# Two attentions: each pair of heads is divided by its softmax sums and stored in two token halves

## The chip, the core and the metric

The kernel runs on one core of a Trainium2 chip. The metric is the time of one execution in microseconds (us); lower is better. Engines: PE is TensorE, DVE is VectorE, ACT is ScalarE, POOL is GpSimd, SP is SyncE, which here only issues DMA transfers.

## What is computed

The reference is a trunk of two layers over 1024 tokens of width 1024, in float32. Layer 0 mixes tokens by a causal attention with 12 heads of 64 (queries and keys from low-rank projections, with a rotary part of 32); layer 1 by a gated linear recurrence. Both layers also attend with 4 heads of 64 to a bank of 256 memory rows. What matters here:

```python
p = jax.nn.softmax(sc, axis=-1).astype(v.dtype)
return jnp.einsum('bhqk,bkhd->bqhd', p, v)            # causal attention, layer 0
...
mem_out = memory_attention(q_mem, mem_k, mem_v)       # both layers
y = jnp.concatenate([tok, mem_out], axis=-1) * jax.nn.silu(gate)
h = layer_norm(ALPHA * h + y @ w_out[layer], ln_g[layer], ln_b[layer])
```

## The kernel before

Matrices are split into a high and a low part, and a product is three matmuls (high x high, high x low, low x high). Activations lie transposed: 128 features on the partitions, 1024 tokens along the free axis. A pair of heads (2 x 64 features) fills one 128x1024 tile `gt`, which holds SiLU(gate) at first and is multiplied by the attention's output in place.

**Attention units.** `attn_unit` makes one unit: up to 512 queries (one half of the tokens, `c` = 0 or 1) against one block of 128 keys. Its front computes scores on PE (L657, or L765 and L766 for the memory), ACT takes the exponential twice (L561 in full, L562 as the high part `ph`), and L564 subtracts to get the low part `pl`, on POOL, or on DVE for one unit in four and for the last memory head. Its back multiplies by V on PE (L572); a 65th column of ones in V gives the sum of the exponentials. `run_units` lets three units' fronts run ahead of a unit's back, and puts other work between them as fills: the projections of the next pair (L113 to L115, with copies L402 and L403), the pass over the next heads' scores that finds each row's maximum (L454 on PE, L456 and L459 on DVE), and near the end the memory's work (L746, L748). A head of layer 0 has 10 units, 3 of them for the first token half and 7 for the second; a pair of heads has 20. A memory head has 4 units, two for each half.

**Finishing.** After the last unit of a half, `finish_chunk` multiplies the unnormalised output into `gt` (L621, DVE) and copies the row of sums to `den` (L622, ACT). When both halves of both heads of a pair are there, `finish_pair` makes the division: two DMAs spread the sums over 128 partitions (L627), DVE takes reciprocals (L628), two DMAs write them to DRAM (L630), two DMAs read them back, each broadcast over 64 partitions (L633), and POOL multiplies the whole `gt` by them (L634). In layer 0 `gt` is then stored to `y_d` (L665; L773 for the first memory pair) and the next gate is loaded into the tile (L667). There are ten pairs: six of layer 0's attention (0 to 5 below), and two of the memory in each layer.

**Order.** The framework puts the instructions into one queue for each engine, in an order from a planner that simulates the program with estimated costs; an engine works its queue in that order, and an instruction that waits holds up all behind it. SP's queue issues all but a few DMAs. Semaphores follow the data by region.

**Around it.** Layer 0's output projection `out_proj` reads `y_d` back by token blocks of 128 (L835, L947) and takes the last memory pair straight from its tile; layer 1's output projection reads the tiles in SBUF.

Of the kernel before, what the change touches and what calls it, by code (L numbers as in the profile page):

```python
# [10 lines left out]
F32 = mybir.dt.float32  # L11
# [4 lines left out]
ALU = mybir.AluOpType  # L16
# [4 lines left out]
S = 1024  # L21
# [23 lines left out]
def hybrid_kernel(ctx: ExitStack, tc: tile.TileContext, io):  # L45
    nc = tc.nc
    PE, ACT, DVE, POOL, SP = nc.tensor, nc.scalar, nc.vector, nc.gpsimd, nc.sync

    main = ctx.enter_context(tc.tile_pool(name="main", bufs=1))
    small = ctx.enter_context(tc.tile_pool(name="small", bufs=2))  # L50
# [192 lines left out]
    y_d = dram.tile([8, 128, S], F32, name="y_d")  # L243
# [9 lines left out]
    HALF = [slice(0, 512), slice(512, 1024)]  # L253
# [243 lines left out]
    den = pb[1].tile([128, S], F32, name="den")  # L497
    den_d = dram.tile([16, 2, S], F32, name="den_d")
# [4 lines left out]
    def vview(t):  # L503
        return t.rearrange("p (s e d) -> p s e d", s=8, e=2)
# [113 lines left out]
    def finish_chunk(gt, e, c, ops):  # L618
        cs = slice(c * 512, (c + 1) * 512)
        y = gt[e * 64:(e + 1) * 64, cs]  # L620
        DVE.tensor_tensor(out=y, in0=ops[0:64, :], in1=y, op=ALU.mult)  # L621
        ACT.copy(den[32 * e:32 * e + 1, cs], ops[64:65, :])  # L622

    def finish_pair(gt, slot):
        rn = small.tile([128, 16], F32, tag="rn", name="rn")
        for e in range(2):
            SP.dma_start(rn[:, e * 8:(e + 1) * 8], den[32 * e:32 * e + 1, :].rearrange("o (a b) -> o a b", a=128))  # L627
        DVE.reciprocal(rn, rn)  # L628
        for e in range(2):
            SP.dma_start(den_d[slot, e].rearrange("(a b) -> a b", a=128), rn[:, e * 8:(e + 1) * 8])  # L630
        rec = Of[slot % 2]
        for e in range(2):
            SP.dma_start(rec[e * 64:(e + 1) * 64, :], den_d[slot, e:e + 1, :].broadcast_to([64, S]))  # L633
        POOL.tensor_tensor(out=gt, in0=gt, in1=rec, op=ALU.mult)  # L634

    SC = 1.0 / math.sqrt(96.0)

    def main_head(h):
        kh_, kl_, qh_, ql_ = sets[h % 4]
        p, e = h // 2, h % 2  # L640
        vh, vl = vview(VH[p % 3]), vview(VL[p % 3])
        gt = GA[p % 4]
        out_units = []
        for c in range(2):
            ops = bank[3 + c]
            units = [([(j, 0, 512, 0)], 512, []) for j in range(4 * c)]
            j = 4 * c
            units.append(([(j, 0, 512, 0)], 512, [0]))
            units.append(([(j + 1, 0, 384, 128), (j + 3, 384, 128, 384)], 512, [0, 384]))
            units.append(([(j + 2, 0, 256, 256)], 256, [0]))  # L650
            for ui, (tl, n, blocks) in enumerate(units):
                def scores(ps, tl=tl, c=c):
                    for (j, c0, w, q0) in tl:
                        ks = slice(j * 128, (j + 1) * 128)
                        qs = slice(c * 512 + q0, c * 512 + q0 + w)
                        for i, (k, q, r) in enumerate(((kh_, ql_, 96), (kl_, qh_, 96), (kh_, qh_, 97))):
                            yield lambda: PE.matmul(ps[:, c0:c0 + w], k[0:r, ks], q[0:r, qs],  # L657
                                                    start=(i == 0), stop=(i == 2))
                last = ui == len(units) - 1

                def post(c=c, ops=ops):
                    finish_chunk(gt, e, c, ops)
                    if c == 1 and e == 1:
                        finish_pair(gt, p)
                        SP.dma_start(y_d[p], gt)  # L665
                        if p < 4:
                            SP.dma_start(gt, gate_d[p])  # L667
                out_units.append(attn_unit(scores, n, SC, blocks,
                                           [(vh[:, j, e, :], vl[:, j, e, :], c0, w, q0) for (j, c0, w, q0) in tl],
                                           ui == 0, last, ops, post if last else None))  # L670
        return out_units
# [82 lines left out]
    def mem_main(m, q1, q2, KH, KL, VmH, VmL, slot, gts, opsb):  # L754
        vh = VmH[:, 0:520].rearrange("p (t h d) -> p t h d", t=2, h=4)
        vl = VmL[:, 0:520].rearrange("p (t h d) -> p t h d", t=2, h=4)
        gt = gts[m // 2]
        out_units = []
        for c in range(2):
            ops = opsb[(2 * m + c) % len(opsb)]  # L760
            qs = slice(c * 512, (c + 1) * 512)
            for kt in range(2):
                def scores(ps, kt=kt, qs=qs):
                    ks = slice(m * 256 + kt * 128, m * 256 + (kt + 1) * 128)
                    yield lambda: PE.matmul(ps, KH[:, ks], q1[:, qs], start=True, stop=False)  # L765
                    yield lambda: PE.matmul(ps, KL[0:65, ks], q2[0:65, qs], start=False, stop=True)  # L766

                def post(c=c, ops=ops):
                    finish_chunk(gt, m % 2, c, ops)
                    if m % 2 == 1 and c == 1:  # L770
                        finish_pair(gt, slot + m // 2)
                        if slot == 6 and m == 1:
                            SP.dma_start(y_d[6], gt)  # L773
                out_units.append(attn_unit(scores, 512, 0.125, [], [(vh[:, kt, m, :], vl[:, kt, m, :], 0, 512, 0)],
                                           kt == 0, kt == 1, ops, post if kt == 1 else None, m == 3))
        return out_units
# [329 lines left out]
    den = pd[1].tile([128, S], F32, name="den1")  # L1106
# [112 lines left out]
```

## Time and profile before

| | us |
|---|---|
| median of 3 runs | 925.75 (925.34 to 928.98) |
| the profiled execution, whole | 924.84 |
| its span, first to last instruction | 923.0 |
| PE busy in the span | 896.5 |
| DVE, ACT, POOL busy | 592.2, 443.1, 222.9 |

Layer 0's attention with the memory lies at 220 to 514 us of the span, layer 1's memory attention at about 745 to 816 us. A line of a timeline has start, duration, engine, line, operation, tile written<-tiles read, shapes, a count xN of merged instructions, and in brackets the idle time before it and what ended it. A busy PE is a modelled figure: consecutive matmuls overlap, so the distance between starts says more than the durations.

### The profile page before, as it was taken

How to read it: one execution, taken by the hardware profiler on the slowest of the kernel's cores; microseconds unless marked ns; L12 is line 12 of the kernel's file. 1: busy time of each engine (PE TensorE's matmuls, PEld its weight loads, DVE VectorE, ACT ScalarE, POOL GpSimd, SP SyncE). 2: the span in 40 equal slices, each digit the busy share in tenths (PEclk: the TensorE clock that was granted, in tenths of full speed). 3: DMA queues.
4: the chain of work that ended last, by engine and by line, in shares of the span. 5: the costliest groups of instructions: out<-in, count | busy, mean ns of one | idle time of the engine just before them, and what ended most of it. 6: DMA issues, size and time to landing. Idle time of an engine off the chain costs nothing.

```text
span 923.0 us, 12452 instructions
## 1 busy us (share of the span) xinstructions
PE 896.5 (97%) x4477; PEld 735.2 (80%) x4477; DVE 592.2 (64%) x1207; ACT 443.1 (48%) x764; POOL 222.9 (24%) x219
## 2 busy tenths in 40 slices
PE   9999999999999999999999999988999999999996
PEld 8998888877787788778777888867888877678886
DVE  7953346258867767796775497646997154457655
ACT  4422311217676667777795122107997156753000
POOL 5100023101526364563672200000000032210000
PEclk9999999999999999999999999998999999999998
DMA  9103133314022213056657653111113921252411
GB/s 328 45 15 109 55 100 127 128 63 111 23 61 70 59 58 104 13 144 178 194 150 207 197 194 125 50 51 47 45 46 113 220 69 47 69 184 91 155 73 46
DMA packets 45945, 96.08 MB, mean 104 GB/s; under 512 B 10906, under 2 KB 20282, under 8 KB 45884
## 3 DMA queue, kind: packets, MB, share of 16 engines
q1 hardware_dynamic: 45308, 94.47, 32.7%
q8 instruction: 35, 0.57, 0.3%
q10 hardware_dynamic: 576, 0.82, 0.3%
q14 instruction: 26, 0.21, 0.1%
HBM read 71.94 MB, written 23.16 MB: 103 GB/s over the span
## 4 chain that ended last, share of the span: by engine, by line
PE 82%; DVE 7%; ACT 3%; issue 3%; DMA 2%; POOL 2%; SPq 0%; DVEq 0%; ACTq 0%; POOLq 0%
PE bank L113 10%; PE bank L115 10%; PE bank L114 10%; PE bank L858 6%; PE bank L860 6%; PE bank L859 6%; PE bank L572 6%; PE bank L657 5%; PE bank L367 3%; PE bank L369 3%; PE bank L368 3%; PE bank L154 2%; PE bank L155 2%; PE bank L153 2%; PE bank L454 2%
## 5 line engine op out<-in xcount | busy, mean ns | idle before, releaser
L564 POOL TENSOR_TENSOR pl<-Pf,ph 128x512 fp32r<-128x512 f32 (+1 forms) x99 | 124.6, 1268 | 116.4 <-ACT ph L562 93.6
L561 ACT ACTIVATE Pf<-bank 128x512 f32<-128x512 f32 (+1 forms) x152 | 86.3, 568 | 50.3 <-DVE bank L558 20.8
L657 PE MATMUL bank<-st,st 96*128 96x512 f32 (+7 forms) x432 | 105.5, 342 | 0.1
L90 DVE TENSOR_TENSOR R<-wf,R 128x1024 fp32r<-128x1024 f32 (+4 forms) x43 | 48.8, 1138 | 65.6 <-POOL R L82 59.8
L657 PEld LDWEIGHTS bank<-st,st 96*128 96x128 f32 (+1 forms) x432 | 75.7, 189 | 13.0 <-DVE st L403 0.5
L562 ACT ACTIVATE ph<-bank 128x512 fp32r<-128x512 f32 (+1 forms) x136 | 76.2, 561 | 0.2
L82 POOL TENSOR_SCALAR R<-wf 128x1024 fp32r<-128x1024 f32 (+3 forms) x25 | 24.4, 979 | 200.1 <-PE bank L114 97.3
L113 PE MATMUL bank<-R,R 128*128 128x256 f32 (+1 forms) x190 | 63.2, 333 | 0.7 <-ACT Pf L375 0.4
L114 PE MATMUL bank<-R,R 128*128 128x256 f32 (+1 forms) x190 | 62.3, 328 | 0.1
L115 PE MATMUL bank<-R,R 128*128 128x256 f32 (+1 forms) x190 | 62.2, 327 | 0.0
L456 DVE CUSTOM_DVE_ANT_0 bank<-bank,cmask 128x384 f32<-128x384 f32 (+3 forms) x96 | 48.8, 517 | 9.8 <-PE bank L454 9.0
L123 ACT ACTIVATE rq_t<-lnv 128x1 f32<-128x1 f32 x16 | 3.3, 203 | 101.7 <-DVE lnv L909 101.7
L367 PE MATMUL bank<-xh,R 128*128 128x512 f32 x128 | 50.8, 397 | 0.1
L369 PE MATMUL bank<-xh,R 128*128 128x512 f32 x128 | 50.7, 396 | 0.0
L368 PE MATMUL bank<-xl,R 128*128 128x512 f32 x128 | 50.5, 395 | 0.0
L572 PE MATMUL bank<-ph,VH 128*65 128x512 f32 (+2 forms) x144 | 49.2, 342 | 0.0
L572 PE MATMUL bank<-pl,VH 128*65 128x512 f32 (+2 forms) x144 | 44.8, 338 | 2.2 <-POOL pl L564 1.2
L572 PE MATMUL bank<-ph,VL 128*65 128x512 f32 (+2 forms) x144 | 47.0, 337 | 0.0
L859 PE MATMUL bank<-wo,yh 128*128 128x512 f32 (+1 forms) x126 | 46.8, 371 | 0.0
L858 PE MATMUL bank<-wo,yh 128*128 128x512 f32 (+1 forms) x126 | 46.6, 369 | 0.0
L860 PE MATMUL bank<-wo,yl 128*128 128x512 f32 (+1 forms) x126 | 46.0, 369 | 0.0
L904 DVE SCALAR_TENSOR_TENSOR GA<-GA,bank 128x512 f32<-128x512 f32 (+1 forms) x34 | 22.0, 647 | 37.1 <-PE bank L860 37.1
(315 smaller groups left out, 2447.1 us busy)
## 6 DMA issues: line engine op xcount, KB each, us to landing
wf<-w SPq DMA_DIRECT2D x26, 512.0 KB
wf<-wout SPq DMA_DIRECT2D x16, 512.0 KB
Of<-den_d SPq DMA_DIRECT2D x20, 256.0 KB
GA<-x SPq DMA_DIRECT2D x8, 512.0 KB
h_d<-GA SPq DMA_DIRECT2D x8, 512.0 KB
GA<-h_d SPq DMA_DIRECT2D x8, 512.0 KB
y_d<-GA SPq DMA_DIRECT2D x7, 512.0 KB
out<-GA SPq DMA_DIRECT2D x7, 512.0 KB
```

The costliest lines, as they stand in the source:

```text
L113: PE.matmul(out, lh, rh, start=(i == 0), stop=False)
L114: PE.matmul(out, lh, rl, start=False, stop=False)
L115: PE.matmul(out, ll, rh, start=False, stop=(i == n - 1))
L367: PE.matmul(ps[n], hi[:, ks], xh[k][:, cs], start=(k == 0), stop=False)
L369: PE.matmul(ps[n], lo[:, ks], xh[k][:, cs], start=False, stop=(k == 7))
L561: ACT.activation(pf[:, :n], ps[:, :n], AF.Exp, scale=scale)
L564: lo_eng.tensor_tensor(out=lo[:, :n], in0=pf[:, :n], in1=f32(hi)[:, :n], op=ALU.subtract)
L572: mm.append(lambda: PE.matmul(ops[0:65, q0:q0 + w], st, mv[:, c0:c0 + w], start=start, stop=stop))
L657: yield lambda: PE.matmul(ps[:, c0:c0 + w], k[0:r, ks], q[0:r, qs], start=(i == 0), stop=(i == 2))
L858: PE.matmul(out, hi, woh[k][:, ns], start=(k == ko[0]), stop=False)
L859: PE.matmul(out, hi, wol[k][:, ns], start=False, stop=False)
L860: PE.matmul(out, lo, woh[k][:, ns], start=False, stop=(k == ko[7]))
```

## The change

`finish_pair` becomes `finish_half`, called after each half of the pair's second head, for that half alone. All six DMAs, the reciprocal and the multiply act on half the tokens, and the store to `y_d` too; the gate load after it stays whole and comes after the second half.

```diff
-    def finish_pair(gt, slot):
-        rn = small.tile([128, 16], F32, tag="rn", name="rn")
+    def finish_half(gt, slot, c):
+        cs = HALF[c]
+        rn = small.tile([128, 8], F32, tag="rn", name="rn")
         for e in range(2):
-            SP.dma_start(rn[:, e * 8:(e + 1) * 8], den[32 * e:32 * e + 1, :].rearrange("o (a b) -> o a b", a=128))
+            SP.dma_start(rn[:, e * 4:(e + 1) * 4], den[32 * e:32 * e + 1, cs].rearrange("o (a b) -> o a b", a=128))
         DVE.reciprocal(rn, rn)
         for e in range(2):
-            SP.dma_start(den_d[slot, e].rearrange("(a b) -> a b", a=128), rn[:, e * 8:(e + 1) * 8])
+            SP.dma_start(den_d[slot, e, cs].rearrange("(a b) -> a b", a=128), rn[:, e * 4:(e + 1) * 4])
         rec = Of[slot % 2]
         for e in range(2):
-            SP.dma_start(rec[e * 64:(e + 1) * 64, :], den_d[slot, e:e + 1, :].broadcast_to([64, S]))
-        POOL.tensor_tensor(out=gt, in0=gt, in1=rec, op=ALU.mult)
+            SP.dma_start(rec[e * 64:(e + 1) * 64, cs], den_d[slot, e:e + 1, cs].broadcast_to([64, 512]))
+        eng = POOL
+        eng.tensor_tensor(out=gt[:, cs], in0=gt[:, cs], in1=rec[:, cs], op=ALU.mult)
...
                     finish_chunk(gt, e, c, ops)
-                    if c == 1 and e == 1:
-                        finish_pair(gt, p)
-                        SP.dma_start(y_d[p], gt)
-                        if p < 4:
+                    if e == 1:
+                        finish_half(gt, p, c)
+                        SP.dma_start(y_d[p][:, HALF[c]], gt[:, HALF[c]])
+                        if c == 1 and p < 4:
                             SP.dma_start(gt, gate_d[p])
...
                     finish_chunk(gt, m % 2, c, ops)
-                    if m % 2 == 1 and c == 1:
-                        finish_pair(gt, slot + m // 2)
+                    if m % 2 == 1:
+                        finish_half(gt, slot + m // 2, c)
                         if slot == 6 and m == 1:
-                            SP.dma_start(y_d[6], gt)
+                            SP.dma_start(y_d[6][:, HALF[c]], gt[:, HALF[c]])
```

## Rows read from the trace of the kernel before

**Rows 1.** The page's part 1: each engine's busy us, share, instructions.

```profile
PE 896.5 (97%) x4477; PEld 735.2 (80%) x4477; DVE 592.2 (64%) x1207; ACT 443.1 (48%) x764; POOL 222.9 (24%) x219
```

**Rows 2.** Windows: bounds, length, busy time by engine, granted clock, DMA share, GB/s.

```profile
238.00:514.00 276.00, 269.73 (x1526) 219.04 (x1525) 199.58 (x452) 196.84 (x372) 138.98 (x122) 1.00 0.38 111
...
800.00:840.00 40.00, 38.75 (x166) 30.09 (x165) 26.12 (x26) 24.74 (x30) 4.61 (x2) 1.00 0.52 174
```

**Rows 3.** Timeline of PE: matmuls that PE stood idle before, and some neighbours.

```profile
315.93 0.39 PE L454 MATMUL bank<-st,st 96*128 96x256 f32 x1 [0.96 <-DVE mx L459]
...
409.78 0.39 PE L572 MATMUL bank<-ph,VL 128*65 128x512 f32 x1
411.16 0.44 PE L572 MATMUL bank<-pl,VH 128*65 128x512 f32 x1 [1.00 <-POOL pl L564]
...
448.39 0.44 PE L572 MATMUL bank<-pl,VH 128*65 128x512 f32 x1 [1.04 <-POOL mx L741]
...
462.42 0.39 PE L572 MATMUL bank<-ph,VL 128*65 128x512 f32 x1
462.65 0.39 PE L572 MATMUL bank<-pl,VH 128*65 128x512 f32 x1
...
485.76 0.44 PE L572 MATMUL bank<-pl,R 128*65 128x512 f32 x1 [1.07 <-POOL pl L564]
...
802.65 0.45 PE L572 MATMUL bank<-mpl,VH 128*65 128x512 f32 x1 [1.25 <-DVE mpl L564]
```

**Rows 4.** The division's multiply, L634, by source line: min/median/max ns.

```profile
L634 POOL TENSOR_TENSOR GA<-GA,Of x8: 2389/2404/2416, 277.2 to 512.8; 128x1024 f32<-128x1024 f32 x8
```

**Rows 5.** Timeline of POOL in layer 0's attention, and at 800 us.

```profile
262.20 1.30 POOL L564 TENSOR_TENSOR pl<-Pf,ph 128x512 fp32r<-128x512 f32 x1 [5.41 <-ACT ph L562]
...
407.49 2.39 POOL L634 TENSOR_TENSOR GA<-GA,Of 128x1024 f32<-128x1024 f32 x1
409.84 3.94 POOL L564 TENSOR_TENSOR pl<-Pf,ph 128x512 fp32r<-128x512 f32 x3
...
428.15 1.30 POOL L564 TENSOR_TENSOR pl<-Pf,ph 128x512 fp32r<-128x512 f32 x1 [3.47 <-ACT ph L562]
...
461.17 3.76 POOL L564 TENSOR_TENSOR pl<-Pf,ph 128x512 fp32r<-128x512 f32 x3 [2.02 <-PE bank L572]
...
479.83 2.41 POOL L634 TENSOR_TENSOR GA<-GA,Of 128x1024 f32<-128x1024 f32 x1 [3.25 <-issue]
...
799.67 2.39 POOL L634 TENSOR_TENSOR GB<-GB,Of 128x1024 f32<-128x1024 f32 x1 [6.86 <-DMA Of<-den_d]
```

**Rows 6.** Timeline of ACT: sums copied after a second head's first half; end of layer 0.

```profile
250.31 0.58 ACT L622 COPY den<-bank 1x512 f32<-1x512 f32 x1
...
458.75 0.58 ACT L622 COPY den<-bank 1x512 f32<-1x512 f32 x1
...
515.26 0.50 ACT L84 CAST R<-GA 128x128 fp32r<-128x128 f32 x2 [1.33 <-POOL GA L634]
```

**Rows 7.** Timeline of SP's queue over pair 3's division.

```profile
396.54 0.55 SPq L627 DMA_DIRECT2D rn<-den  x1
399.26 0.81 SPq L630 DMA_DIRECT2D den_d<-rn  x2
400.72 1.13 SPq L633 DMA_DIRECT2D Of<-den_d  x2
...
409.91 0.33 SPq L665 DMA_DIRECT2D y_d<-GA  x1
```

**Rows 8.** The reciprocal, L628, by source line: durations, then DVE's idle time before.

```profile
L628 DVE RECIPROCAL rn<-rn x10: 235/252/253, 269.7 to 809.1; 128x16 f32<-128x16 f32 x10
...
  DMA rn<-den: 6.3, 5
```

**Rows 9.** Timeline of DVE: a reciprocal of pair 1, and layer 1's memory.

```profile
315.28 0.25 DVE L628 RECIPROCAL rn<-rn 128x16 f32<-128x16 f32 x1 [0.81 <-DMA rn<-den]
...
800.55 2.65 DVE L564 TENSOR_TENSOR mpl<-Pf,mph 128x512 fp32r<-128x512 f32 x2 [1.79 <-ACT mph L562]
```

## The prediction

> **What bounds the kernel now.** I read the page first, then windows over the two stages that the diff touches, then PE's timeline in them for the places where PE stands idle, and at each of these the timelines of POOL, DVE, ACT and SP for the instruction that was late.
>
> The page shows one engine at its limit: PE is busy 897 of 923 us, and no other above 64% [rows 1]. In the stage from 238 to 514 us PE is idle 276.00 - 269.73 = 6.3 us, and in the 40 us around the end of layer 1's memory attention 1.25 us, at a granted clock of 1.00 in both, the level of 2.4 GHz [rows 2]. So whatever the change does to POOL, DVE or SP, it gains at most these 7.5 us (0.8%), and it costs only where it makes PE wait anew. The question is which of these idle stretches hang on the division of a pair.
>
> Matmuls of 512 columns follow each other at 0.23 us (462.42 and 462.65), though each is drawn 0.39 long [rows 3]. So a stall costs the distance of starts less 0.23: at 411.16 it is 411.16 - 409.78 - 0.23 = 1.15 us, 0.15 more than the idle time in brackets. Read in the same way, the stalls that stand next to a division are 1.15 (pair 3), 1.19 (pair 4, 448.39), 1.22 (pair 5, 485.76), 1.40 (layer 1, 802.65) and 1.11 (pair 1, 315.93) [rows 3]. Together 6.1 us.
>
> They have three causes. In pairs 3, 4 and 5 the matmul waits for a low part that POOL made late, and before it in POOL's queue stands the multiply L634: 407.49 for 2.39 us, then three low parts without a break; 479.83 for 2.41 us [rows 5]. In layer 1 the low part is DVE's: the first of two takes 2.65 - 0.69 = 1.96 us, while POOL's multiply runs from 799.67 to 802.06 [rows 5, 9]. In pair 1 it is DVE's reciprocal, which waits 0.81 us for its sums to land, with the maximum pass behind it on DVE [rows 9].
>
> **The change, part by part.**
>
> *The second half's multiply is half as long.* It stays where the whole one was, and lasts about 1.3 us in place of 2.40 [rows 4]; the nearest row is a POOL tensor_tensor of 128x512, 1.30 us [rows 5]. A low part queued behind it comes 1.1 us earlier. That takes 1.1 us from each of the stalls of pairs 3, 4 and 5, which leaves 0.05 to 0.12 of each: -3.3 us. The bounds are -3.6 (the stalls go whole, because the broadcasts land earlier too) and 0 (the planner puts the multiply elsewhere, and other low parts wait behind it).
>
> *Layer 1.* The multiply splits into two of 1.3 us. The first half's sums are there some 4 us earlier, so its multiply falls before the busy stretch; the second would run from about 799 to 800.3 and be over before DVE's low part at 800.55. The bounds are -1.4 and 0; I take -1.0, since a low part may still meet the end of a POOL instruction. The Trainium skill, page "SBUF — State Buffer", section "Who interferes with whom", says that a DVE instruction with two SBUF inputs and a GpSimd instruction that reads SBUF exclude each other for a whole instruction. By that rule DVE's low part would be held until 802.06 and end at 802.75, which the trace supports roughly (it ended near 802.5); halves would shorten one such hold but offer twice as many, and by it alone this term would lie anywhere between its bounds.
>
> *The first half's multiply, new, ten times.* Where does it fall? The chain from the last DMA of the sums to the multiply took 407.49 - 396.54 = 10.9 us in pair 3 [rows 5, 7]; with halves I reckon some 10. The second head's first half is complete at unit 15 of 20: its sums are copied by 250.9 in pair 0 [rows 6], so the multiply is due near 261, and there POOL has nothing to do for 5.41 us, as PE is busy with the next pair's projections and no exponentials come [rows 5]. Pairs 1 to 4 have the same hole, the last and shortest one 3.47 us before 428.15 [rows 5]. The multiply costs nothing there: the cover is the hole, and without it it would cost its own 1.3 us each. Pair 5 has no such hole: its sums are copied by 459.3 [rows 6], and after 461.17 POOL makes three low parts in one go, the first of them done at about 462.5, 0.2 us before the matmul that wants it at 462.65 [rows 3, 5]. The multiply comes near 470, where the margins are still thin. I take +0.8 us, between 0 (it slips behind the next fill) and 2.4 (it costs its length and waits another 1.1 us on a late broadcast). In the memory pairs of layer 0 POOL is idle around the divisions, so 0.
>
> *The reciprocal, ten more on DVE.* Each lasts 0.25 us and may wait for its sums at the head of DVE's queue; behind it stand the maximum pass and the low parts. Of ten so far five waited, 6.3 us in all [rows 8], and one cost PE anything, 1.11 us. Ten more would cost +1.0 on the same rate. The bounds are 0 and 10 x 1.1 = +11.
>
> *Issues on SP, 60 more and 7 more stores.* About 0.5 us each; the six of a division occupy SP for 0.55 x 2 + 0.81 + 1.13 = 3.0 us of some 13 [rows 7]. SP also stands still between them until each step has landed. What is queued behind are weights and rotary rows for the next pair, which it wants several us later. PE has no stall of note that ends on such a load now. I take 0, up to +2.
>
> *End of layer 0.* The last pair's multiply ends at 515.2, and ACT waited 1.33 us for it [rows 6]. PE did not stop there, because three token blocks were prepared ahead. An earlier first half only adds margin: 0.
>
> The sum is -3.3 - 1.0 + 0.8 + 1.0 = -2.5 us, from the profiled 924.84 to 922.3. The median of the runs lies 0.9 us above that execution, so 923.2.
>
> **The rivals.**
>
> *Every stall goes and nothing new comes.* Then -3.6 - 1.4 - 1.1 (pair 1's reciprocal no longer meets the maximum pass) = -6.1, which gives 919.6. For it: POOL's holes lie just where the first halves fall. Against it: it needs luck on DVE in ten new places.
>
> *The waits only move.* The second half's chain still has all its legs, so POOL still stands at the multiply until the broadcast lands (3.25 us idle before 479.83 [rows 5]), and the planner, which does not know the real landing times, puts a low part behind each of the two. If half of the gain goes that way (-2.1) and pair 5 and DVE cost 2.4 and 1.5, the time is 924.84 + 0.9 + 1.8 = 927.5.
>
> *Slower: the reciprocals block DVE.* The new ones come at units 15 to 19 of a pair, where the maximum pass uses DVE most, and each stands at the head of the queue until a DMA has landed, as at 315.28 [rows 9]. At 1.1 us each, ten cost 11 us against gains of 4.3, and the time is 932.4. It decides from about 0.9 us each. Against it: nine of ten cost PE nothing so far. The Trainium skill, page "DMA: Bandwidth & Descriptors", section "Rules for kernel authors", says that many small transfers should be joined into a large one, since below 64 KB one pays mostly overhead. Here the sums' transfers of 4 KB become 2 KB, so by that rule each half would wait about as long as the whole did, and there would be twice as many waits; no run so far shows the half.
>
> **How the numbers follow.** Chances: the forecast 0.50, every stall gone 0.20, the waits move 0.18, the reciprocals 0.12. A measurement of this kernel tells about 0.5% (4.6 us) from no change. The forecast's own range, 921.1 to 926, and the moved waits lie within it; only the first rival is below 921.1, only the last above 930.4: faster 0.20, same 0.68, slower 0.12. The range runs from the first rival's 919.6 to 929, the moved waits' time with SP's share added to it, and leaves the last rival out.
>
> **What would show it.** Twenty multiplies at about 1.3 us; the first halves' multiplies of pairs 0 to 4 in the holes after the pair's last low part; PE's stalls near 411, 448 and 486 gone or below 0.2, and the one near 802 smaller; one new stall near 465 to 472. The prediction is wrong if stalls stay as long with a multiply half as long (then the landing, not POOL's work, set them), if PE stalls before L454 behind reciprocals in more than two or three pairs, or if SP's queue delays weights so that L113 waits.

## The result

The changed kernel is slower: a median of 940.71 us (938.63 to 942.90, 4 runs) against 927.17 for the kernel before on the same chip (4 runs), a ratio of 1.0146, 95% interval 1.011 to 1.0183. The prediction was 923.2, range 919.6 to 929.0: wrong in sign, and outside its range. The profiled execution took 938.63 us, span 936.8, 13.8 more than before.

The page of the changed kernel, part 1 and the count of DMA packets (45945 before):

```profile
PE 902.3 (96%) x4477; PEld 737.2 (79%) x4477; DVE 592.3 (63%) x1217; ACT 442.5 (47%) x764; POOL 221.8 (24%) x229
...
DMA packets 54314, 96.09 MB, mean 103 GB/s; under 512 B 17098, under 2 KB 26474, under 8 KB 54252
```

PE's 4477 matmuls are the same; it was busy 5.8 us longer for them and idle 8.0 us more (34.5 against 26.5) [rows 1]. To find where, I compare when PE had done the same number of matmul columns in both traces:

| stretch of the kernel before | what it holds | later by then | in the stretch |
|---|---|---|---|
| up to 400 | | 0.1 | 0.1 |
| 400 to 420 | pair 3 | 4.3 | +4.2 |
| 440 to 480 | pairs 4 and 5 | 7.0 | +2.7 |
| 480 to 520 | memory pairs, first matmuls of the output projection | 12.8 | +5.8 |
| 520 to 800 | | 11.9 | -0.9 |
| 800 to 820 | layer 1's first memory pair | 10.6 | -1.3 |
| 820 to 840 | layer 1's output projection begins | 14.4 | +3.8 |

So three places make most of the loss, the stretch from 440 to 480 adds 2.7 us, and one place gains. In the stretch from 520 to 800 the granted clock was at half for 6.8 us in this execution and for 10.2 us in that of before, which is part of its -0.9. Windows over the three, columns as in [rows 2]:

```profile
400.00:420.00 20.00, 17.50 (x84) 13.65 (x83) 15.73 (x41) 11.09 (x22) 11.91 (x11) 0.83 0.62 163
...
500.00:520.00 20.00, 16.29 (x66) 11.85 (x65) 7.68 (x12) 5.77 (x10) 2.16 (x4) 0.91 0.64 176
830.00:850.00 20.00, 17.88 (x71) 14.00 (x70) 13.91 (x14) 13.84 (x15) 1.30 (x1) 0.91 0.67 228
```

Each has idle time of PE and a granted clock below 1.00. PE's timeline there:

```profile
411.72 0.64 PE L454 MATMUL bank<-st,st 96*128 96x320 f32 x1 [2.44 <-DVE mx L456]
...
508.28 0.50 PE L860 MATMUL bank<-VH,R 128*128 128x512 f32 x1 [3.71 <-ACT R L84]
...
840.58 0.55 PE L860 MATMUL bank<-wo,yh 128*128 128x512 f32 x1 [2.12 <-ACT yh L84]
```

The granted clock is 0.50 (the 1.2 GHz level) from 410.8 us on, within the first wait, for 6.8 us, and behind the other two, from 509.8 and 840.9 us on, for 3.4 us each.

**Near 411.** PE's score pass L454 waits for DVE's maximum pass L456. DVE's timeline, first of the changed kernel, then of the one before:

```profile
405.76 1.84 DVE L90 TENSOR_TENSOR R<-wf,R 128x1024 fp32r<-128x1024 f32 x1
...
409.91 1.23 DVE L90 TENSOR_TENSOR R<-wf,R 128x1024 fp32r<-128x1024 f32 x1 [1.97 <-ACT R L84]
411.05 0.56 DVE L456 CUSTOM_DVE_ANT_0 bank<-bank,cmask 128x384 f32<-128x384 f32 x1
```

```profile
407.20 0.57 DVE L456 CUSTOM_DVE_ANT_0 bank<-bank,cmask 128x384 f32<-128x384 f32 x1
...
413.65 1.22 DVE L90 TENSOR_TENSOR R<-wf,R 128x1024 fp32r<-128x1024 f32 x1
```

In the changed kernel a second split of memory tokens (L90) stands ahead of L456; it waits for ACT's conversion of the loaded tile, which itself waited 2.10 us for the load and ended at 409.88 (408.75 before). Before, this split comes after L456, at 413.65. No line of the diff touches it: the planner moved it, and with it some of PE's and ACT's instructions between 407 and 411.

**Near 508.** PE's first matmul of the output projection waits for ACT to convert a tile read back from `y_d`. ACT's timeline, then SP's, changed kernel:

```profile
507.61 0.62 ACT L84 CAST R<-R 128x512 fp32r<-128x512 f32 x1 [1.71 <-DMA R<-y_d]
```

```profile
500.78 0.34 SPq L775 DMA_DIRECT2D y_d<-GA  x1
501.58 1.09 SPq L634 DMA_DIRECT2D Of<-den_d  x2
502.77 0.53 SPq L734 DMA_DIRECT2D mem_d<-R  x1
...
503.82 0.49 SPq L837 DMA_DIRECT2D R<-y_d  x1
506.42 0.33 SPq L775 DMA_DIRECT2D y_d<-GA  x1
506.84 0.99 SPq L837 DMA_DIRECT2D R<-y_d  x2
```

The load that PE waits for is the first, at 503.82. It stands behind the store of the first half, which waits for POOL's multiply (499.22 to 500.75), behind the second half's read-back, which waits for the reciprocals to land, and behind a store to `mem_d`, which waits for POOL too. The last two loads go out 0.42 us behind the store of the second half, which waits for POOL's multiply (505.13 to 506.39); what they feed is converted later, and PE has no stall over 0.4 us behind it. SP's timeline before:

```profile
490.12 1.99 SPq L835 DMA_DIRECT2D R<-y_d  x2
492.20 1.11 SPq L633 DMA_DIRECT2D Of<-den_d  x2
```

There the third load followed at 494.57, and the store L773 after it, at 500.83.

**Near 840.** PE waits for ACT's conversion of `yh`, and ACT's timeline shows it queued behind a conversion of weights that waited 4.51 us for its load. SP's timeline shows that load behind another, into the tile that POOL's last multiply (830.09 to 831.39) reads:

```profile
837.08 1.05 ACT L84 CAST wo<-wf 128x1024 fp32r<-128x1024 f32 x1 [4.51 <-DMA wf<-wout]
...
839.48 2.93 ACT L84 CAST yh<-GA 128x1024 fp32r<-128x1024 f32 x3
```

```profile
831.42 0.33 SPq L852 DMA_DIRECT2D Of<-ln_b  x1
831.85 9.63 SPq L785 DMA_DIRECT2D wf<-wout  x4
```

What the prediction said of the multiply did come, and the reciprocals cost PE nothing new. Both by source line, with DVE's idle time before the second, and PE behind pair 1's reciprocal (0.96 us idle before, [rows 3]):

```profile
L636 POOL TENSOR_TENSOR GA<-GA,Of x16: 1262/1291/1528, 258.8 to 521.5; 128x512 f32<-128x512 f32 x16
```

```profile
L629 DVE RECIPROCAL rn<-rn x20: 150/202/203, 252.5 to 819.7; 128x8 f32<-128x8 f32 x20
...
  DMA rn<-den: 5.8, 9
```

```profile
315.52 0.39 PE L454 MATMUL bank<-st,st 96*128 96x256 f32 x1 [0.99 <-DVE mx L459]
```

### The profile page after: what moved, and what is told of

Read it like the earlier page. It is cut to its first block, busy times and chain, and to the rows that moved or that the text cites. A ratio compares the mean times of both kernels' runs of the same rounds, so it can differ in the third digit from the quotient of the medians.

```text
span 936.8 us, 12607 instructions
## 1 busy us (share of the span) xinstructions
PE 902.3 (96%) x4477; PEld 737.2 (79%) x4477; DVE 592.3 (63%) x1217; ACT 442.5 (47%) x764; POOL 221.8 (24%) x229
## 4 chain that ended last, share of the span: by engine, by line
PE 81%; DVE 6%; DMA 5%; ACT 4%; issue 2%; POOL 1%; SPq 0%; POOLq 0%; ACTq 0%; DVEq 0%
PE bank L113 9%; PE bank L115 9%; PE bank L114 9%; PE bank L572 7%; PE bank L860 6%; PE bank L862 6%; PE bank L861 6%; PE bank L659 5%; PE bank L367 3%; PE bank L368 3%; PE bank L369 3%; PE bank L454 2%; PE bank L154 2%; PE bank L155 2%; PE bank L153 2%
## 5 line engine op out<-in xcount | busy, mean ns | idle before, releaser
L564 POOL TENSOR_TENSOR pl<-Pf,ph 128x512 fp32r<-128x512 f32 (+1 forms) x99 | 120.8, 1229 | 92.7 <-ACT ph L562 83.4
L90 DVE TENSOR_TENSOR R<-wf,R 128x1024 fp32r<-128x1024 f32 (+4 forms) x43 | 48.8, 1139 | 70.3 <-POOL R L82 60.2
L456 DVE CUSTOM_DVE_ANT_0 bank<-bank,cmask 128x384 f32<-128x384 f32 (+3 forms) x96 | 48.8, 518 | 12.1 <-PE bank L454 11.3
```

The source lines that it names most:

```text
L564: lo_eng.tensor_tensor(out=lo[:, :n], in0=pf[:, :n], in1=f32(hi)[:, :n], op=ALU.subtract)
```

## The experiments

Theory A: the halved work is cheap; the time goes where SP's queue, worked in order, puts a load late behind the added steps, or where the planner puts a waiting instruction ahead of one that PE needs. It goes at a few places. Rival B: each pair in halves costs something everywhere, by its added issues and waits.

All kernels are the one before with a list of the pairs that are finished in halves. Pairs 0 to 5 are layer 0's attention, 6 and 7 its memory, 8 and 9 layer 1's memory.

```diff
+    HALVES = (0, 1, 2, 3, 4, 5)
...
-                    if c == 1 and e == 1:
+                    if e == 1 and p in HALVES:
+                        finish_half(gt, p, c)
+                        SP.dma_start(y_d[p][:, HALF[c]], gt[:, HALF[c]])
+                    elif e == 1 and c == 1:
                         finish_pair(gt, p)
```

**Which pairs cost.** Three kernels with a part of the list, and one whose memory pairs' six division DMAs are issued by POOL.

```diff
+    HALVES = (0, 1, 2, 3, 4, 5)
```

> Halves in the six pairs of layer 0's attention alone; the memory pairs are divided whole, as before. Theory A (three separate places: a stall of PE before a maximum-pass matmul near 411 us with the half clock behind it, thin margins at 440 to 482 us, and the two out-projections' starts): this kernel keeps the first two, 4.2 + 2.7 us, so 932 to 935 where before takes 926 to 928, and no long stall before L858-type matmuls of either output projection. Rival B (every added division costs about the same, by its DMAs and waits): six tenths of 13.5 us, +8 us, spread evenly over 250 to 480 us. Rival C (only the whole combination hurts): within 2 us of before.

```diff
+    HALVES = (6, 7)
```

> Halves in layer 0's two memory pairs alone. Theory A: the memory weights, the tokens' y tiles or both wait in SP's queue behind the halves' steps, the first output projection starts late, and PE's clock drops behind that stall: +3 to +5.5 us, all of it at 480 to 515 us. Rival B: two tenths of 13.5, +2.7 us. Rival C: within 2 us of before.

```diff
+    HALVES = (8, 9)
```

> Halves in layer 1's two memory pairs alone. Theory A: PE's stall of 1.25 us behind DVE's low part goes (-1.3 us), the output weights' loads wait in SP's queue, the second output projection stalls some 2 us behind the y split on ACT, and with the half clock behind it costs 3.8: +2.5 us in all. Rival B: +2.7 us with no such stall. Rival C: -1.3 us, the gain alone.

```diff
+    HALVES = (6, 7, 8, 9)
...
+        Q = POOL
...
+            Q.dma_start(rn[:, e * 4:(e + 1) * 4], den[32 * e:32 * e + 1, cs].rearrange("o (a b) -> o a b", a=128))
```

> Halves in the four memory pairs, with their DMAs issued from POOL's queue in place of SP's (the stores to y_d stay on SP). Theory A, with SP's queue as the cause in both memory stages: both output projections start without the stalls of 3.7 and 2.1 us, and the time is 0 to 2 us below before. If it is not SP's order but the later end of the chains themselves, or the planner's other order, the stalls stay: the sum of the two kernels with halves in one memory stage each, +5 to +8 us.

| pairs in halves | median us | kernel before | ratio, 95% interval |
|---|---|---|---|
| 0 to 5 | 931.62 | 925.03 | 1.0093 (1.0058 to 1.0128) |
| 6, 7 | 931.53 | 925.03 | 1.0075 (1.006 to 1.009) |
| 8, 9 | 924.62 | 925.03 | 0.999 (0.9971 to 1.0009) |
| 6 to 9, division DMAs on POOL | 945.35 | 925.03 | 1.0223 (1.0197 to 1.0249) |

The sum of the first three, 6.6 + 6.5 - 0.4 = 12.7, is near the whole change's 13.5, but by place the losses do not add up: by PE's progress, pairs 0 to 5 lose 2.4 us near 411, 3.3 between 440 and 480 and 2.6 at the output projection, and pairs 6 and 7 another 6.4 there, where the whole change lost 4.2, 2.7 and 5.8. Rival B's +8 us for pairs 0 to 5 is not far from the total, but none of it lies before 400 us. Theory A's sizes were off in all four: 931.62 lies 0.4 below its range, with a stall of 1.99 us at 523.56 that it ruled out; +6.5 was forecast as 3 to 5.5; -0.4 as +2.5 (1.2 gained at 800 to 820, 1.8 lost behind it, no half clock); and the division on POOL as 0 to 2 us below before, where +20.3 also lies far outside the other forecast.

Pairs 6 and 7 alone show the stall at the output projection. PE's and SP's timelines of that kernel:

```profile
502.72 0.79 PE L880 MATMUL bank<-VH,R 128*128 128x512 f32 x1 [4.58 <-ACT R L84]
```

```profile
497.07 0.45 SPq L857 DMA_DIRECT2D R<-y_d  x1
501.23 0.33 SPq L791 DMA_DIRECT2D y_d<-GA  x1
501.61 1.04 SPq L857 DMA_DIRECT2D R<-y_d  x2
```

Here too PE waits for the first load, at 497.07: the conversion that it feeds starts at 502.05.

On POOL's queue the same DMAs did worse. The output projection then waited 4.43 us at 526.53, and in layer 1 PE waited 9.91 us at 848.31, behind output weights for which ACT had waited 10.09 us. There POOL's multiplies, of which the last ended at 838.70, stand in one queue with the DMAs that they wait for, and the weights go out behind the last one, at 839.15. That the division leaves SP is not enough.

**The load behind the store.** Two kernels: pairs 6 and 7 in halves with the three loads of `y_d` issued by ACT; and the changed kernel with the half stores issued by POOL.

```diff
-        SP.dma_start(f32(t).rearrange("p (k t) -> p k t", k=4), y_d[0:4, :, sl].rearrange("k p t -> p k t"))
+        ACT.dma_start(f32(t).rearrange("p (k t) -> p k t", k=4), y_d[0:4, :, sl].rearrange("k p t -> p k t"))
```

> As the kernel with halves in layer 0's memory pairs alone, with the three loads of the tokens' y tiles ahead of the first output projection issued from ACT's queue in place of SP's. Theory A (these loads were late because they stood in SP's queue behind the halves' transfers and the stores that wait for the multiply): the stall of 4.6 us and the half clock after it go, 6 to 7 us, so 925 to 926. Rival (the loads are late because their buffers come free late, or the DMA engines are full): the stall stays over 3 us.

```diff
-                        SP.dma_start(y_d[p][:, HALF[c]], gt[:, HALF[c]])
+                        POOL.dma_start(y_d[p][:, HALF[c]], gt[:, HALF[c]])
...
-                            SP.dma_start(y_d[6][:, HALF[c]], gt[:, HALF[c]])
+                            POOL.dma_start(y_d[6][:, HALF[c]], gt[:, HALF[c]])
```

> The changed kernel, with the half stores to y_d issued from POOL's queue, right behind the multiply, in place of SP's. If the stores are what blocks SP (each waits there for POOL's multiply), the loads behind them come earlier, the stall at the first output projection shrinks by 2 us or more, and the time is 934 to 938. If the other waits in SP's queue (the sums' landing, the reciprocal, the broadcast) are enough, it stays at 939 to 942.

With the loads on ACT: 925.01 us (10 runs) against 925.19, ratio 0.9997 (0.9981 to 1.0014). The whole 6.5 us is gone, though every other DMA of the halves stayed on SP. The window of the output projection's start shows it, with SP's loads and with ACT's, and so do the loads by source line.

```profile
494.00:514.00 20.00, 14.90 (x54) 10.44 (x53) 8.02 (x12) 6.90 (x13) 1.36 (x3) 0.83 0.62 172
```

```profile
494.00:514.00 20.00, 19.59 (x84) 14.72 (x83) 7.85 (x13) 6.88 (x12) 2.62 (x2) 1.00 0.71 183
```

```profile
L857 ACTq DMA_DIRECT2D R<-y_d x3: 375/390/400, 490.2 to 498.8; - x3
```

With the stores on POOL: 936.89 (934.72 to 940.18) against 925.19, ratio 1.0112 (1.0082 to 1.0142): 11.7 us above the kernel before on the same chip, where the whole change lies 13.5 above. That is within the forecast for stores that block SP. The stall of the output projection is gone there too, and the 5.8 us lost between 480 and 520 become -0.6. But the run does not show that the stores alone did it: the first load goes out at 501.17 in place of 503.82, now ahead of the read-back (503.06), and PE is itself 3.5 us later at 480 us than in the changed kernel, so that the load has that much more time. For between 460 and 480 a new 7.9 us appears. DVE's, POOL's and PE's timelines:

```profile
472.47 5.75 DVE L564 TENSOR_TENSOR pl<-Pf,ph 128x512 fp32r<-128x512 f32 x1 [0.71 <-ACT ph L562]
478.15 1.27 DVE L766 TENSOR_REDUCE mx<-bank 128x2 f32<-128x512 f32 x2
```

```profile
472.68 2.51 POOL L564 TENSOR_TENSOR pl<-Pf,ph 128x512 fp32r<-128x512 f32 x2
...
475.19 2.47 POOL L564 TENSOR_TENSOR pl<-Pf,ph 128x512 fp32r<-128x512 f32 x2
```

```profile
478.88 0.79 PE L764 MATMUL bank<-R,st 128*128 128x256 f32 x2 [3.72 <-DVE mx L766]
```

A DVE instruction that takes 0.69 us elsewhere ends only when POOL's four low parts are through, the memory's maximum pass starts behind it, and PE waits for that.

**The moved split.** Three kernels: pairs 0 to 5 with the split's DVE part held to its place in the program; pairs 0 to 2, where the split stays behind L456 and PE's and ACT's orders are those of before; and pair 3 alone, where the split is moved.

```diff
-            wsplit(wf[j % 2], R[i], R[2 + i])
+            hi_copy(weng[0], R[i], wf[j % 2])
+            tc.keep_in_program_order(DVE.tensor_tensor(out=R[2 + i], in0=wf[j % 2], in1=f32(R[i]), op=ALU.subtract))
```

> As the kernel with halves in layer 0's attention alone, with one pin: on DVE the split of the two memory-token loads keeps its place behind the maximum pass written before it. Theory A (near 411 us PE stalls because the planner moved the second of these splits, which waits for its load to land, ahead of the maximum pass on DVE): the stall of 1.8 us and the half clock after it go, and about 2.3 us with them, so 929 to 930 where the kernel without the pin takes 931.6, if the rest of the order stays harmless. Rival (the reciprocals or the first half's multiply block there): the stall stays at 1.5 us or more.

```diff
+    HALVES = (0,1,2,)
```

> Halves in the first three main pairs of layer 0 only; the order of PE and ACT is then that of the kernel before, and on DVE the maximum passes near 411 us stand ahead of the memory tokens' split, as before. Theory A (the loss near 411 us is the moved split, which comes from the fourth pair alone): 924 to 926, no growth of the stall near 411, no half clock there. Theory B (each pair's 7 more issues on SP make loads late wherever they are): three pairs of ten, 13.5 x 0.3 = 4, so 928 to 930.

```diff
+    HALVES = (3,)
```

> Halves in the fourth main pair of layer 0 only. On DVE two splits of the memory tokens then stand ahead of the maximum pass near 411 us, one of which comes after it in the kernel before. Theory A: a stall of PE of 1.8 to 2.5 us near 411 with half clock behind it, 2.3 to 4.2 us at that place, so 927 to 930 with what little comes later. Theory B (issues on SP): one pair of ten, 1.4, so 926 to 927, with no stall over 1 us near 411.

Held in place: 942.38 us against 925.19, ratio 1.0166 (1.0145 to 1.0187), a clear miss of 929 to 930. The stall near 411 did go (L456 runs at 408.65, ahead of the split, and PE does not wait), but the planner placed the splits of the memory's weights and much else anew. PE's timeline has waits elsewhere, among them:

```profile
440.77 0.39 PE L113 MATMUL bank<-R,R 128*128 128x256 f32 x1 [0.84 <-ACT R L84]
...
510.05 0.69 PE L572 MATMUL bank<-pl,R 128*65 128x512 f32 x1 [2.56 <-DVE pl L564]
```

So this run supports the site's cause but does not isolate it, since PE's and ACT's orders differ from about 392 us on, and it gives no price; one place held fixed is not the rest left alone.

Pairs 0 to 2: 924.75 (12 runs) against 925.23, ratio 0.9992 (0.9978 to 1.0006). Three pairs in halves, with 18 more division DMAs and 3 more stores on SP, cost nothing that these runs tell. That rules out B's price for these pairs.

Pair 3 alone: 928.87 (12 runs) against 925.23, ratio 1.0032 (1.0014 to 1.0049), within A's forecast. The same split stands ahead of L456, and PE waits. DVE's and PE's timelines:

```profile
408.48 1.75 DVE L90 TENSOR_TENSOR R<-wf,R 128x1024 fp32r<-128x1024 f32 x1 [0.84 <-ACT R L84]
410.15 0.55 DVE L456 CUSTOM_DVE_ANT_0 bank<-bank,cmask 128x384 f32<-128x384 f32 x1
```

```profile
410.82 0.42 PE L454 MATMUL bank<-st,st 96*128 96x320 f32 x1 [1.70 <-DVE mx L456]
...
434.23 0.39 PE L113 MATMUL bank<-R,R 128*128 128x256 f32 x1 [1.28 <-ACT R L84]
```

In this execution the clock did not fall near 411; a stall of before at that place (1.15) was saved, so the place itself cost 0.5 and the rest of the 3.5 us came later, at 434 and after. One pair's halves suffice to change the order.

**Versions that keep what pays.** Layer 1's first memory pair alone; that and pair 4; and six pairs, with the `y_d` loads on ACT.

```diff
+    HALVES = (8,)
```

> Halves in one pair alone, the first memory pair of layer 1; all other nine whole. Theory A: PE's stall of 1.25 us behind DVE's low part goes and nothing else changes, since the order on PE and ACT is that of before: 1.3 us below before, within what 3 rounds tell from it. Rival B (each added division costs 0.7 to 1.4 us by its DMAs): equal to before or slower.

```diff
+    HALVES = (4,8,)
```

> Halves in the fifth main pair of layer 0 and the first memory pair of layer 1 only: the two places whose stalls before (1.0 at 448.39, 1.2 at 802.65) stood behind a long multiply; the order on PE stays that of the kernel before. Theory A (the multiply in halves gains what it blocked, and costs nothing where the order stays): 925.2 less 1.9, as measured with the memory pair alone, less up to 1.0: 922 to 923.5. Theory B (each pair costs 1.4 in issues): 925 to 926.

```diff
+    HALVES = (0,1,2,6,7,8,)
...
-        SP.dma_start(f32(t).rearrange("p (k t) -> p k t", k=4), y_d[0:4, :, sl].rearrange("k p t -> p k t"))
+        ACT.dma_start(f32(t).rearrange("p (k t) -> p k t", k=4), y_d[0:4, :, sl].rearrange("k p t -> p k t"))
```

> Halves in six of the ten pairs (the first three main pairs and both memory pairs of layer 0, the first memory pair of layer 1), with the three y tile loads on ACT's queue as in the run of layer 0's memory pairs; PE's order stays that of the kernel before. Theory A (a pair in halves costs nothing where neither the planner's order nor a later load is moved): 925.2 with -1.9 from the memory pair of layer 1 and up to -0.7 from the first three, 0 from layer 0's memory pairs: 922.5 to 924. Theory B (each pair costs 1.4 in issues on SP): 925.2 + 6 x 1.4 - 1.9 = 931 to 933.

Pair 8 alone: 923.26 (921.97 to 924.18, 6 runs) against 925.19, ratio 0.9961 (0.994 to 0.9982). It is the lowest median here, 1.9 us below before, where theory A said 1.3. The stall that stood at 802.65 is gone, since the second half's multiply on POOL is over before DVE's low part starts:

```profile
798.77 1.28 POOL L649 TENSOR_TENSOR GB<-GB,Of 128x512 f32<-128x512 f32 x1 [2.96 <-DMA Of<-den_d]
```

```profile
800.32 0.69 DVE L564 TENSOR_TENSOR mpl<-Pf,mph 128x512 fp32r<-128x512 f32 x1 [1.79 <-ACT mph L562]
```

Pair 9 is what eats this gain. Its two halves are complete close together (in the changed kernel its last three rows of sums are copied at 813.34, 815.05 and 817.07), so both chains share SP: with pairs 8 and 9 the last multiply starts at 817.36 and ends at 818.65, with pair 8 alone the whole multiply starts at 813.95 and ends at 816.74, earlier though twice as long. Behind it wait a load into the same tile and, in SP's queue, the weights: they go out at 819.75 against 818.87, and PE waits where it did not with pair 8 alone:

```profile
828.11 0.50 PE L880 MATMUL bank<-wo,yh 128*128 128x512 f32 x1 [1.61 <-ACT yh L84]
```

Pairs 4 and 8: 927.99 (12 runs) against 925.23, ratio 1.003 (1.0012 to 1.0047). Theory A's forecast of 922 to 923.5 failed, and so did B's of 925 to 926: PE's order being that of before was not enough. PE's, ACT's and SP's timelines, and SP's of the kernel before, show the other half of the mechanism:

```profile
446.63 0.62 PE L672 MATMUL bank<-st,st 96*128 96x256 f32 x3 [1.39 <-ACT ph L562]
```

```profile
443.81 1.05 ACT L84 CAST VH<-wf 128x1024 fp32r<-128x1024 f32 x1 [2.66 <-DMA wf<-wout]
```

```profile
430.66 0.32 SPq L680 DMA_DIRECT2D y_d<-GA  x1
...
431.53 1.05 SPq L805 DMA_DIRECT2D wf<-wout  x2
...
438.94 0.33 SPq L805 DMA_DIRECT2D wf<-wout  x1
```

```profile
426.58 5.17 SPq L783 DMA_DIRECT2D wf<-wout  x2
...
434.10 0.50 SPq L783 DMA_DIRECT2D wf<-wout  x1
```

The first half's store waits for POOL's multiply (429.34 to 430.64), and the loads of output weights behind it go out at 431.53 and after; before, the first of them went out at 426.58. The load at 438.94 (434.10 before) waits until DVE has split the one two before it, in the same buffer (437.73 to 438.91). ACT stands at its conversion, with the exponentials that PE waits for queued behind it. This costs some 4.4 us between 440 and 460, half clock for 3.4 us included. The changed kernel lost 1.2 us in that stretch, at full clock.

Six pairs: 924.76 (12 runs) against 924.76, ratio 0.9995 (0.998 to 1.001). It misses A's 922.5 to 924 by 0.8 and B's 931 to 933 by more than 6. The trace keeps the 1.2 us gain at 802, and loses 2.1 us at a new wait of 1.55 us at 532.91, where PE waits for DVE's split of a tile of the output projection. In DVE's queue that split stands behind one of weights before which DVE was idle for 5.17 us; what brought it there was not tried.

## Why the prediction was wrong

*The steps that failed.* "Issues on SP, 60 more and 7 more stores ... I take 0, up to +2" is the first. I looked for loads on which PE already stalled and found none, but not at how much margin each load had, nor at what a step waits for when it stands in the queue. A store waits for its multiply, and a multiply for a read-back; a load behind them waits for all three. Moving three loads away from SP gave back the 6.5 us of pairs 6 and 7. Moving the stores left 1.8 us of gain in all, and does not tell what a store alone costs. The prediction did name weights held up in SP's queue as a sign of being wrong, but priced SP's share at 2 us at most: here late loads are most of the 5.8 us at the first output projection and the 3.8 us at the second.

"End of layer 0. An earlier first half only adds margin: 0" is the same mistake at one place. The data are ready earlier, but the loads of `y_d` for the token blocks prepared ahead now stand behind the first half's store and the second half's read-back: +5.8 us.

*A term that was missing.* I kept every instruction where it was and put in the new ones. The planner did not: the split ahead of L456 cost 4.2 us in the changed kernel with the clock's share. The prediction named the planner only for the multiply.

*What a stall costs.* I counted the gap alone. Around 2.44, 3.71 and 2.12 us the clock was at half for 6.8, 3.4 and 3.4 us, of which 5.9, 3.4 and 3.4 lay behind the gap. Where PE is the bound half of that is lost, 3.0, 1.7 and 1.7 us; with the gaps, less the 1.15 saved near 411, this makes 4.2, 5.4 and 3.8 us, as measured at the three places but for 0.4.

*What held.* Twenty multiplies at 1.29 us (reckoned 1.3); those of first halves in POOL's holes, as at 258.83 in pair 0 and 431.75 in pair 4. Layer 1's term, -1.0, measured 1.2 to 1.3 in the traces and 1.9 in the medians. The stalls of pairs 3 to 5 did go in their old form: PE's waits for POOL's low parts fell from 2.2 us (longest 1.1) to 1.2 (longest 0.5), but later waits took that up. The new reciprocals cost 0, not 1.0: nine of twenty waited 5.8 us together, but up to 400 us PE is 0.1 later, and its one stall over 0.4 us behind a reciprocal is the old one of pair 1, 0.99 us. With that the slower rival falls; the outcome was slower, but not for the reason on which its chance of 0.12 stood. Of the rivals, "the waits only move" was nearest in kind, at 927.5, and 13 us too low.

*Two rules beside the runs.* By the Trainium skill, "SBUF — State Buffer", section "Who interferes with whom", a DVE instruction with two SBUF inputs and a GpSimd instruction that reads SBUF exclude each other. The runs agree in the main: before, DVE's low part runs from 800.55 to 802.60 (2.05 us, where the prediction reckoned 1.96 from two merged) beside a multiply that ends at 802.06, and with pair 8 alone, where the multiply is over by 800.05, the one at 800.32 takes its 0.69 us. By the Trainium skill, "DMA: Bandwidth & Descriptors", section "Rules for kernel authors", small transfers should be joined. Here 18 more of them, in pairs 0 to 2, cost nothing that the runs tell.

*What stays open.* The 2.7 us between 440 and 480 are not taken apart in the whole change; with pair 4 (and 8) in halves the loss there was 4.7, with another stall. Near 508 it is shown that the loads' place in SP's queue costs the time, not which of the steps ahead of them. Near 840 that pair 9's halves cost it is shown by pair 8 alone; that the weights' place in the queue does is read from the trace. How pair 3's first half leads the planner to another order was not tried.

## What to carry over

Before splitting a step into halves, list for each queue what stands behind the new steps and how much earlier than needed it lands; a store that waits for compute, or a load into a tile that the compute still reads, makes the loads behind it in the queue wait for that compute. Split only where the finished half is wanted or where the long instruction blocks something: one pair of ten was shown to pay here. Where a planner sets the order, compare the orders of all engines before and after, since an edit moves instructions that it does not touch.

## What the hardware showed beside

The granted clock did not follow a stall's length simply: behind 1.70 us (pair 3 alone) and 1.61 us (pairs 8 and 9) it stayed at 1.00, behind 1.39 us with 0.82 two us later (pairs 4 and 8) it was at half for 3.4 us, and around 4.58 us (pairs 6 and 7) for 6.8. It also differs between executions of one kernel: the twelve of pair 3 alone ran from 925.82 us at a mean clock of 0.995 to 932.64 at 0.988.

With the stores on POOL one DVE instruction is drawn from 472.47 to 478.22, 5.75 us for 0.69 of work, while POOL made four low parts in a row from 472.68 to 477.66. The rule on the shared port tells of a hold for one instruction (the Trainium skill, "SBUF — State Buffer", section "Who interferes with whom"); here the waiting engine did not get in between two.
